# Encoder layer start: projections of half the tokens taken on unscaled x, first weight loaded in halves, third projection pair ahead of the memory's

## The chip, the cores and the metric

The kernel runs on one core of one Trainium2 chip. The metric is the device time of one execution in microseconds (us), as the median of several runs. Matrix products run on TensorE (PE, with PEld for its weight loads), elementwise work on VectorE (DVE), ScalarE (ACT) and GpSimd (POOL), and SyncE (SP) issues most of the loads.

## The reference, cut to what matters

Two encoder layers act on x (512 tokens by 1024). Each begins with a root-mean-square norm and one large input projection that feeds neighbourhood attention (A), dilated attention (B) and attention into 256 memory tokens (M):

```python
mem_n = rms_norm(mem, mem_norm_g)
for l in range(DEPTH):
    h = rms_norm(x, g_pre_mix[l])          # x * rsqrt(mean(x*x) + eps) * g
    proj = h @ w_in[l]
    q_a, k_a, v_a, q_b, k_b, v_b, q_m, gate_pre = jnp.split(proj, splits, axis=-1)
    ...
    o_m = memory_attention(q_m, mem_n, w_mem_kv[l])
    ...
```

The factor `rsqrt(mean(x*x) + eps)` is one number for each token. It can therefore be applied to h before the product or to a token's column of the product behind it. The change rests on that.

## The kernel before, in words

x lies transposed in SBUF: 8 tiles (k = 0 to 7) of 128 features, and the 512 tokens stand along the row, in two halves of 256 (`HALVES`). Every fp32 operand is split in two parts, hi (a cast by ACT, `split`, L225) and lo (a subtraction by DVE or POOL), and one product becomes three matmuls (`mm3`, L257): hi by hi, hi by lo, lo by hi. A projection of 128 output features has 8 tiles k, so it is 24 matmuls over 512 tokens, or 24 over each half of 256.

The order of TensorE's work is fixed by hand. `Woven` (L46) keeps a clock in units of TensorE work. Side jobs such as norms, softmax steps and attention heads are generators with due times on that clock, and they are put between the matmuls of the main line whenever they fall due (`tick`) or are asked for (`need`). The engines then work through their instructions in that program order and wait on semaphores, so a matmul whose operand is late holds up every matmul behind it.

At the start of layer 0 the order is this. `load_x` (L195) issues the four loads of the first half of x on SP's queue, then two weights of 512 KB follow (`group_weights`, L504), then the second half of x, the vectors and four more weights. `idle` (L883) gives TensorE products without use before data is there. `first_squares` (L871) squares a half of x on ACT and adds pairs on DVE. `rstd_job` (L334) sums the squares over the features by matmuls with a column of 1/1024, takes the square root on ACT and the reciprocal on DVE, and spreads the factor over the partitions with two transposes. `pre_norm_job` (L373) then makes h for each k: one DVE operation with x, gain and factor (`normed`, L354), the cast on ACT, the subtraction on DVE. Only then do the projections of that half start (`run_group`, L510): six weights, by pairs, into six PSUM banks, first for half 0 and then for half 1. The norm of half 1 is made beside the products of half 0. `mem_norm_job` (L460) does the same for the memory, and `mem_kv` (L488) takes its four products of 24 matmuls over 256 columns. Behind them come the third pair's projections (`proj`, L525, for `pr == 2`), with the six heads of attention A woven in (`attention_job`, L773; `a_head_job`, L608). The weights of `proj` and `mem_kv` go through two buffers for hi and two for lo (`weights`, L230).

In the profile L255 is the line of all matmuls, L266 and L351 are transposes, and L114 is the line of all DVE and ACT instructions, since a helper issues them. Tile names: `o`, `pt`, `mm`, `s` are PSUM banks, `h` and `ka` hold parts of h or x, `m` and `whi`/`wlo` hold parts of weights, `wraw` a weight as loaded, `y` squares or softmax rows.

Of the kernel before, what the change touches and what calls it, by code (L numbers as in the profile page):

```python
# [1 line left out]

# [117 lines left out]
def tile_hybrid_encoder(ctx, tc, xT, memT, memg, vecs, rpb, w_in, w_kv, w_bra, w_brb, w_brm,  # L120
# [20 lines left out]
    def nm(s):  # L141
        uid[0] += 1
        return f"{s}_{uid[0]}"
# [14 lines left out]
    def small(tag, bufs, shape=(128, 256)):  # L158
        return tp.tile(list(shape), F32, tag=tag, name=nm(tag), bufs=bufs)
# [42 lines left out]
    load_x(HALVES[0])  # L202
# [27 lines left out]
    def weights(src, K, C, slot=None, eng=None, after=None):  # L230

        raw = wp.tile([128, K, C], F32, tag="wraw", name=nm("wraw"))
# [89 lines left out]
    def sumsq_add(acc, src, first, slot=None, eng=None):  # L322
        if first:
            ACT.activation(acc, src, AF.Square)
        else:
            n = acc.shape[-1]
            sq = slot((128, 256)) if slot else small("sq2", 4) if n == 256 else small("sq", 2, (128, 512))
            ACT.activation(sq, src, AF.Square)
            (eng or V).tensor_add(acc, acc, sq)
# [40 lines left out]
        V.tensor_mul(y, ps, R)  # L370
        return y

    def pre_norm_job(l, goff, acc, hs, i, after=None):  # L373
        half, box = HALVES[i], []
        yield from rstd_job(acc if isinstance(acc, list) else [acc[:, half]], 256, box, after)
        for k in range(KD):
# [80 lines left out]
        return [(htile(), htile()) for _ in range(KD)]  # L457


    def mem_norm_job(l, hm, slot):  # L460
        raws = []
        for k2 in range(KD // 2):
            t = slot(F32, (128, 2, N_MEM))
            nc.scalar.dma_start(out=t, in_=memT[:, 2 * k2:2 * k2 + 2, :])
            raws += [t[:, 0, :], t[:, 1, :]]
        acc = small("h32", 3)
        for k in range(KD):
            sumsq_add(acc, raws[k], k == 0, None, MSQ if l else V)
        yield 14.0
        box = []  # L470
        yield from rstd_job([acc], N_MEM, box)
        for k in range(KD):
            t = slot(F32R, (128, 2, N_MEM))
            normed(raws[k], mg[:, k:k + 1], box[0], t[:, 0, :], t[:, 1, :])
            hm.append((t[:, 0, :], t[:, 1, :]))
        yield 1.2
        wv.give(f"mem{l}")

# [6 lines left out]
        vm.append(t)  # L485
        wv.give(f"vm{l}.{len(vm)}")

    def mem_kv(l, hm, km, vm, pre=()):  # L488
        wv.need(f"mem{l}")
        for m in range(4):  # L490
            w = pre[m] if pre else weights(w_kv[l, m], KD, 128)
# [15 lines left out]
    def group_banks():  # L507
        return [mmbank(), mmbank(), obank(128), tbank(), sbank(), sbank()]
# [13 lines left out]
                    mm3(ps[:, cols or half], w[k], rhs, k == 0, k == n - 1, 256)  # L522
                wv.tick()

    def proj(l, m, hs, after=None):  # L525
        w = weights(w_in[l, m], KD, 128, after=after)
        ps = mmbank()
        linear(ps, w, hs)
        return ps
# [341 lines left out]
    def first_squares(half):  # L871
        sqs = [ytile((128, 256)) for _ in range(KD)]
        for k in range(KD):
            ACT.activation(sqs[k], xh(k, half), AF.Square)
            if k % 2:
                V.tensor_add(sqs[k], sqs[k], sqs[k - 1])
            if k in (3, 5) and half != HALVES[0]:
                V.tensor_add(sqs[k], sqs[k], sqs[k - 2])
        return sqs[1::2] if half == HALVES[0] else sqs[5::2]

    idle_bank = obank(128)

    def idle(n):  # L883

        one, none = mean[:, 0:1], zero[:, 0:1]
        a, b = (bass.AP(t.tensor, t.offset, [list(t.ap[0]), [0, w]]) for t, w in ((one, 128), (none, 512)))
        for _ in range(n):
            mm(idle_bank, a, b, True, True, 0.0)

    idle(2)  # L890
    hs = h_tiles()
    sqs = first_squares(HALVES[0])
    first_copy.clear()
    gw = group_weights([w_in[0, FIRST[0]]], (V,))
    wv.spawn(pre_norm_job(0, V_PRE, sqs, hs, 0, first_copy[0]))
    gw += group_weights([w_in[0, FIRST[1]]], (V,))
# [3 lines left out]
    wv.need(f"h0.{V_PRE}.0")  # L900
    with tc.issue_after(last_copy[0]):
        sqs = first_squares(HALVES[1])
    wv.spawn(pre_norm_job(0, V_PRE, sqs, hs, 1), SD1)
    gw += group_weights([w_in[0, m] for m in FIRST[2:]], (V, G, V, G))
    for t, c in ((tab0, c_tab0), (tab1, c_tab1)):
        nc.sync.dma_start(out=t, in_=c)
    hm = []
    wv.spawn(mem_norm_job(0, hm, big), 6.0)
    km, vm = [], []

    for l in range(depth):
        pss = group_banks()
        run_group((gw, pss), hs, HALVES[0], f"h{l}.{V_PRE}.0")
        if l == 0:
            run_group((gw, pss), hs, HALVES[1], f"h{l}.{V_PRE}.1")
# [9 lines left out]
        qkva, qkvb, qm, oa, ob, om = ([], [], []), ([], [], []), [], [], [], []  # L925
        wv.spawn(attention_job(l, qkva, qkvb, qm, km, vm, oa, ob, om))
        for pr in range(3):
            for i, evac in enumerate((a_q, a_k, a_v)):
                ps = pss[FIRST.index(3 * i + pr)] if pr < 2 else proj(l, 3 * i + pr, hs, fence if i < 2 else None)
                evac(ps, qkva, *([f"va{l}.{pr}"] if i == 2 else []))  # L930
            if pr == 1:
# [202 lines left out]
```

## Time and profile before

| | before |
|---|---|
| median of 3 runs | 1534.44 us (1533.58 to 1535.34) |
| the profiled execution | 1534.84 us, of which 1533.1 us are the span from the first to the last instruction |
| TensorE busy | 1517.0 us, 99% of the span, 7970 matmuls |
| VectorE, ScalarE, GpSimd busy | 939.6, 714.0, 122.0 us |
| granted TensorE clock, mean | 0.996 |
| chain that ended last | PE 98%, DVE 1% |
| first matmul of a projection | 11.88 us after the span's start |

The profile has a page of totals and views that answer questions. In a timeline each row has the start, the duration, the engine, the line and the operation with its output and inputs; behind it stands the idle time before it and what ended that. In the chain of waits a row has the start, the time that passed, and the engine. In the table of stretches each engine has its busy time with its number of instructions, then come the granted TensorE clock, the DMA share and GB/s. In a table of groups the two numbers behind the bar are the busy time in us and the mean duration in ns. TensorE is full from about 27 us on, so what can be gained by order alone lies in front of that; what can be lost lies anywhere.

### The profile page before, as it was taken

The page shows a single profiled execution, that of the slowest core. Times are in us where ns is not written, and L with a number is a line of the kernel's source. Part 1 is how long each engine was busy: PE and PEld are TensorE (multiplying, and loading weights), DVE is VectorE, ACT ScalarE, POOL GpSimd, SP SyncE. Part 2 cuts the span into 40 slices and gives each one's busy share as a digit, 9 for nine tenths or more (in the row PEclk, how much of TensorE's full clock was granted, in tenths as well). Part 3 has the DMA queues.
Part 4 walks back from the last instruction along what each step waited for, and adds up shares of the span by engine and source line. Part 5 has one row for each costly group of instructions (what it writes and reads, how often), then busy time and mean ns, then how long its engine had stood idle before and what let it go on. Part 6 is the DMA issues. An engine that isn't in the chain of part 4 may idle for free.

```text
span 1533.1 us, 20644 instructions
## 1 busy us (share of the span) xinstructions
PE 1517.0 (99%) x7970; PEld 1297.8 (85%) x7970; DVE 939.6 (61%) x1686; ACT 714.0 (47%) x1274; POOL 122.0 (8%) x191
## 2 busy tenths in 40 slices
PE   8999999999999999999999999999999999999997
PEld 7988888888988888888898888888889888888887
DVE  6685666335777777633387856643457877776233
ACT  5565555336544444533366655532364544444231
POOL 3220000220000000010043100012100000000000
PEclk9999999999999999999999999999999999999998
DMA  7231122234112222333362222132340223223331
GB/s 255 95 112 61 62 71 97 83 96 166 55 56 96 96 99 97 118 100 98 115 180 81 87 69 71 59 103 76 117 165 15 96 97 97 96 96 90 100 106 63
DMA packets 47490, 149.23 MB, mean 97 GB/s; under 512 B 5648, under 2 KB 9872, under 8 KB 47392
## 3 DMA queue, kind: packets, MB, share of 16 engines
q1 hardware_dynamic: 43632, 139.46, 27.9%
q0 software_dynamic: 2464, 6.36, 1.6%
q10 hardware_dynamic: 1296, 2.10, 0.5%
q8 instruction: 62, 1.02, 0.3%
q14 instruction: 36, 0.29, 0.1%
HBM read 145.80 MB, written 2.10 MB: 96 GB/s over the span
## 4 chain that ended last, share of the span: by engine, by line
PE 98%; DVE 1%; DMA 0%; SPq 0%; ACT 0%; issue 0%; ACTq 0%
PE mm L255 85%; PE s L255 5%; PE o L255 4%; PE pt L266 2%; PE pt L255 2%; DMA x<-in_xT_dram 0%; DVE y L114 0%; DVE h L114 0%; PE pt L351 0%; DVE m L114 0%; SPq L198 0%; DVE x L114 0%; ACT whi L114 0%; PE s L266 0%; SPq L233 0%
## 5 line engine op out<-in xcount | busy, mean ns | idle before, releaser
L255 PE MATMUL mm<-h,whi 128*128 128x512 f32 x2496 | 775.8, 392 | 0.0
L255 PEld LDWEIGHTS mm<-h,whi 128*128 128x128 f32 x2496 | 461.1, 188 | 91.0
L255 PE MATMUL mm<-h,wlo 128*128 128x512 f32 x1248 | 486.6, 390 | 0.0
L114 DVE TENSOR_TENSOR wlo<-wraw,whi 128x1024 fp32r<-128x1024 f32 (+1 forms) x213 | 258.1, 1212 | 275.8 <-ACT whi L114 273.2
L114 ACT CAST whi<-wraw 128x1024 fp32r<-128x1024 f32 (+1 forms) x213 | 221.2, 1039 | 297.4 <-PE mm L255 284.7
L255 PEld LDWEIGHTS mm<-h,wlo 128*128 128x128 f32 x1248 | 234.2, 188 | 49.5
L255 PE MATMUL mm<-m,whi 128*128 128x512 f32 (+1 forms) x768 | 209.1, 359 | 0.0
L255 PEld LDWEIGHTS mm<-m,whi 128*128 128x128 f32 x768 | 136.9, 189 | 21.6
L255 PE MATMUL mm<-m,wlo 128*128 128x512 f32 (+1 forms) x384 | 137.6, 358 | 0.0
L114 DVE SCALAR_TENSOR_TENSOR y<-y,vec,y 128x511 f32<-128x511 f32 x176 | 130.5, 748 | 3.5 <-ACT y L114 0.9
L114 DVE TENSOR_TENSOR y<-mm,R 128x512 f32<-128x512 f32 x82 | 56.4, 688 | 68.5 <-PE mm L255 68.5
L255 PEld LDWEIGHTS mm<-m,wlo 128*128 128x128 f32 x384 | 72.4, 189 | 10.8
L114 ACT ACTIVATE y<-y,vec 128x512 f32<-128x512 f32 x88 | 71.0, 813 | 2.1 <-DVE y L114 1.9
L808 POOL TENSOR_TENSOR m<-m,y 128x512 f32<-128x512 f32 x28 | 36.1, 1289 | 397.0 <-DVE y L114 397.0
L114 ACT CAST m<-pt 128x512 fp32r<-128x512 f32 (+2 forms) x74 | 39.1, 534 | 49.6 <-PE pt L266 42.5
L114 ACT ACTIVATE y<-y 128x512 f32<-128x512 f32 x44 | 27.8, 632 | 72.3 <-DVE y L114 71.9
L255 PE MATMUL mm<-m,m 128*128 128x512 f32 x240 | 61.5, 393 | 0.0
L114 DVE TENSOR_TENSOR m<-pt,m 128x512 fp32r<-128x512 f32 (+2 forms) x74 | 45.9, 622 | 23.9 <-ACT m L114 23.1
L114 ACT ACTIVATE y<-y,st 128x256 f32<-128x256 f32 (+1 forms) x80 | 43.6, 546 | 30.7 <-DVE st L114 29.7
L114 DVE TENSOR_TENSOR acc<-acc,sq 128x256 f32<-128x256 f32 (+1 forms) x80 | 38.2, 478 | 27.4 <-ACT sq L114 25.5
L114 ACT CAST m<-y 128x512 fp32r<-128x512 f32 x32 | 19.8, 619 | 72.5 <-DVE y L114 72.5
L255 PEld LDWEIGHTS mm<-m,m 128*128 128x128 f32 x240 | 44.2, 188 | 8.8
(161 smaller groups left out, 1778.4 us busy)
## 6 DMA issues: line engine op xcount, KB each, us to landing
wraw<-in_w_in_dram SPq DMA_DIRECT2D x88, 512.0 KB, 3.7
wraw<-in_w_up_dram SPq DMA_DIRECT2D x88, 512.0 KB, 3.7
wraw<-in_w_down_dram SPq DMA_DIRECT2D x32, 512.0 KB, 3.5
wraw<-in_w_out_dram SPq DMA_DIRECT2D x16, 512.0 KB, 3.8
wraw<-in_w_down_dram SPq DMA_DIRECT2D x16, 384.0 KB, 3.1
wraw<-in_w_kv_dram SPq DMA_DIRECT2D x8, 512.0 KB, 4.1
y<-in_rpb_dram POOLq DMA_DIRECT2D x12, 256.0 KB, 3.4
wraw<-in_w_bra_dram SPq DMA_DIRECT2D x16, 192.0 KB, 2.3
```

The costliest lines, as they stand in the source:

```text
L114: return op(*args, **kw)
L255: wv.pe(nc.tensor.matmul(ps, a, b, start=first, stop=last), cost)
L266: wv.pe(nc.tensor.transpose(ps[:, 128 * i:128 * i + 128], s, ident), 0.11)
L808: (V if br == 2 and m >= 6 else G).tensor_add(acc[m], acc[m], gs)
```

## The change

Layer 0 alone is changed, and in it what stands ahead of attention B.

- The first weight is loaded in two halves between the tiles of x (`load_x` with `w`), and the first half of x is multiplied by the gain and split without its norm factor (`lead`). The six projections of half 0 run on these tiles (`raw`). Three products without use stand ahead of them, in place of two.
- The squares of half 0 are made behind the splits of the first four weights, the factor R comes from `factors_job`, and each of the six PSUM results is multiplied by R on DVE (`times_factors`). The fourth to sixth weights are loaded into buffers of other tags, so that all six loads are issued early; all six weights are split by ACT and DVE (before, two of them by ACT and POOL).
- The norm of half 1 is due later (`SDR`), and h of half 0, which the later projections need, is made behind it.
- Half 1 runs its first two weights by pair, as before, then the third pair's weights are loaded (`third`), then the other four. The memory's squares wait for h of half 0 (flag `"tiles"`). The third pair's projections come ahead of `mem_kv`, and the attention job starts after a delay (`KV_TIME`), so that the memory's products now lie among the heads of attention A.

```diff
-SD1 = 4.0
+MD0, SDR, KV_TIME = 8.0, 14.0, 16.4
...
-    def load_x(half):
+    def load_x(half, w=None, src=None):
         for k in range(0, KD, 2):
             i = half.start // 256
             nc.sync.dma_start(out=xs[:, i, k:k + 2, :], in_=xT[i, k // 2])
+            if w is not None and k % 4 == 2:
+                c = slice(k - 2, k + 2)
+                nc.sync.dma_start(out=w[:, c, :], in_=src[:, c, :])
...
-    idle(2)
+    idle(3)
     hs = h_tiles()
-    sqs = first_squares(HALVES[0])
...
+    raw = [(t[:, 0, :], t[:, 1, :]) for t in [ktile(F32R, (128, 2, 256)) for _ in range(KD)]]
+    def lead(n=2):
+        for k in [left.pop(0) for _ in range(n)]:
+            hi, lo = raw[k]
+            ACT.activation(hi, xh(k, HALVES[0]), AF.Copy, scale=g0[:, k:k + 1])
+            V.scalar_tensor_tensor(out=lo, in0=xh(k, HALVES[0]), scalar=g0[:, k:k + 1], in1=f32(hi),
+                                   op0=ALU.mult, op1=ALU.subtract)
+    gw = [[]]
+    for k in (0, 4):
+        lead(4)
+        hi, lo = big(), big()
+        split(w0[:, k:k + 4, :].rearrange("p a b -> p (a b)"), hi, lo)
...
+    for m, where in zip(FIRST[1:4], (("wraw", 3), ("wraw", 3), ("whi", 2))):
+        gw.append(weights(w_in[0, m], KD, 128, big, V, None, where))
     load_x(HALVES[1])
...
+    with tc.issue_after(last_copy[0]):
+        sqs, R = first_squares(HALVES[0]), rtile()
+    wv.spawn(factors_job(), MD0)
...
+    wv.spawn(pre_norm_job(0, V_PRE, sqs1, hs, 1), SDR)
...
+    for i in (0, 2, 4):
+        run_group((gw[i:i + 2], pss[i:i + 2]), raw, FULL, None, HALVES[0], 1 if i == 0 else 2)
+        if i == 2:
+            times_factors(0, low)
+    wv.need(f"h0.{V_PRE}.1")
+    for i in (2, 4):
+        times_factors(i, last_lo[V])
+    wv.spawn(mem_norm_job(0, hm, big, "tiles"), 0.0)
+    wv._step()
+    for k in range(KD):
+        normed(xh(k, HALVES[0]), g0[:, k:k + 1], R[:, HALVES[0]], hs[k][0][:, HALVES[0]], hs[k][1][:, HALVES[0]])
...
         fence = crit[0]
-        if l == 0:
-            mem_kv(l, hm, km, vm)
-        wv.spawn(attention_job(l, qkva, qkvb, qm, km, vm, oa, ob, om))
+        wv.spawn(attention_job(l, qkva, qkvb, qm, km, vm, oa, ob, om), 0.0 if l else KV_TIME)
...
+        if l == 0:
+            mem_kv(l, hm, km, vm, after=fence)
```

Three places show how the order moves. The first is TensorE at the start of the program. In the rows `o` is the bank of the products without use, `pt` that of the sums of squares (`mean,y`) and their transposes (`ident,st`), `mm_283` and `mm_262` the bank of the first projection. Before:

```order
L255 MATMUL o_108<-zero,mean 128x512 x2
L255 MATMUL pt_173<-mean,y_128 128x1 x2
L255 MATMUL pt_173<-mean,y_130 128x1 x2
L255 MATMUL pt_173<-mean,y_132 128x1 x2
L255 MATMUL pt_173<-mean,y_134 128x1 x2
L351 MATMUL pt_173<-ident,st_182 128x128 x2
L255 MATMUL mm_283<-h_111,m_149 128x256
L255 MATMUL mm_283<-h_112,m_149 128x256
L255 MATMUL mm_283<-h_111,m_150 128x256
```

And now:

```order
L260 MATMUL o_111<-zero,mean 128x512 x3
L260 MATMUL mm_262<-ka_131,m_147 128x256 x2
L260 MATMUL mm_262<-ka_131,m_148 128x256
L260 MATMUL mm_262<-ka_132,m_147 128x256 x2
L260 MATMUL mm_262<-ka_132,m_148 128x256
```

The sums of squares of half 0 no longer stand ahead of the first projection; they come 78 matmuls later, inside the second pair of weights.

The second place is DVE ahead of the weights that follow the six projections. `wlo` is the lo part of such a weight: of the memory before, of the third pair now. `h_95` and `h_104` collect the memory's squares, `ka` and `m_587` are evacuations of projections. Before:

```order
L114 TENSOR_TENSOR h_95_393<-h_95_393,sq_101_410 128x256
L114 TENSOR_TENSOR h_95_393<-h_95_393,sq_102_413 128x256
L114 TENSOR_TENSOR wlo_701<-wraw_698,whi_700 128x1024
L114 TENSOR_TENSOR wlo_742<-wraw_739,whi_741 128x1024
L114 RECIPROCAL st_551<-st_551 128x2
```

And now:

```order
L115 TENSOR_TENSOR m_587<-mm_262,m_587 64x512
L115 TENSOR_TENSOR h_104_521<-h_104_521,sq_107_529 128x256
L115 SCALAR_TENSOR_TENSOR ka_595<-mm_263,ka_593 64x512
L115 TENSOR_TENSOR h_104_521<-h_104_521,sq_108_532 128x256
L115 TENSOR_TENSOR wlo_615<-wraw_612,whi_614 128x1024
L115 TENSOR_TENSOR h_104_521<-h_104_521,sq_109_535 128x256
L115 TENSOR_TENSOR wlo_621<-wraw_618,whi_620 128x1024
L115 TENSOR_TENSOR h_104_521<-h_104_521,sq_110_538 128x256
L115 TENSOR_TENSOR m_726<-s_267,m_726 64x512
L115 TENSOR_TENSOR h_104_521<-h_104_521,sq_111_541 128x256
```

The memory's seven adds stood in one run (the last two are shown); they now alternate with evacuations and with the third pair's weights, and all of them stand behind the norm of half 1, the multiplications by R and h of half 0.

The third place is TensorE at the memory's products (`mm_786`, `pt_745` before, `mm_971` now); `s_984` are scores of the first head of attention A. Before:

```order
L255 MATMUL pt_745<-m_598,whi_741 128x256 x2
L255 MATMUL pt_745<-m_598,wlo_742 128x256
L255 MATMUL pt_745<-m_603,whi_741 128x256 x2
L255 MATMUL pt_745<-m_603,wlo_742 128x256
L255 MATMUL mm_786<-m_568,whi_782 128x256 x2
```

And now:

```order
L260 MATMUL mm_971<-m_792,whi_967 128x256 x2
L260 MATMUL mm_971<-m_792,wlo_968 128x256
L260 MATMUL s_984<-ka_592,m_586 128x256
L260 MATMUL s_984<-ka_594,m_586 128x256
L260 MATMUL s_984<-ka_592,m_586 128x256
L260 MATMUL s_984<-ka_594,m_586 128x256
L260 MATMUL mm_971<-m_797,whi_967 128x256 x2
L260 MATMUL mm_971<-m_797,wlo_968 128x256
```

The memory's products stood alone; now the first two heads run among them.

More of the change, by code (lines that the diff above doesn't have):

```diff
@@ L1 @@
+import contextlib
 import heapq
@@ L228, in split, with weights @@
         last_lo[eng or V] = (eng or V).tensor_sub(lo, src, f32(hi)).ins
-    def weights(src, K, C, slot=None, eng=None, after=None):
-        raw = wp.tile([128, K, C], F32, tag="wraw", name=nm("wraw"))
+    def weights(src, K, C, slot=None, eng=None, after=None, where=("wraw", 3)):
+        raw = wp.tile([128, K, C], F32, tag=where[0], name=nm("wraw"), bufs=where[1])
         nc.sync.dma_start(out=raw, in_=src)
@@ L371, in scaled, with pre_norm_job @@
         return y
-    def pre_norm_job(l, goff, acc, hs, i, after=None):
+    def pre_norm_job(l, goff, acc, hs, i, after=None, R=None):
         half, box = HALVES[i], []
         yield from rstd_job(acc if isinstance(acc, list) else [acc[:, half]], 256, box, after)
+        if R is not None:
+            ACT.copy(R[:, half], box[0])
         for k in range(KD):
@@ L465, in mem_norm_job @@
             raws += [t[:, 0, :], t[:, 1, :]]
+        if flag:
+            yield flag
         acc = small("h32", 3)
-        for k in range(KD):
-            sumsq_add(acc, raws[k], k == 0, None, MSQ if l else V)
-        yield 14.0
+        with tc.issue_after(crit[0]) if flag else contextlib.nullcontext():
+            for k in range(KD):
+                sumsq_add(acc, raws[k], k == 0, None, MSQ if l else V)
+        yield 15.5 if flag else 14.0
         box = []
@@ L475, in mem_norm_job @@
             hm.append((t[:, 0, :], t[:, 1, :]))
+        if flag:
+            with tc.issue_after(last_copy[0]):
+                ACT.activation(smalls(1), eps, AF.Exp)
         yield 1.2
@@ L486, in mem_v_job, with mem_kv @@
         wv.give(f"vm{l}.{len(vm)}")
-    def mem_kv(l, hm, km, vm, pre=()):
+    def mem_kv(l, hm, km, vm, pre=(), after=None):
         wv.need(f"mem{l}")
         for m in range(4):
-            w = pre[m] if pre else weights(w_kv[l, m], KD, 128)
+            w = pre[m] if pre else weights(w_kv[l, m], KD, 128, after=after)
             ps = (mmbank if pre or m % 2 == 0 else tbank)((128, N_MEM))
@@ L523, in run_group, with proj @@
                 wv.tick()
-    def proj(l, m, hs, after=None):
-        w = weights(w_in[l, m], KD, 128, after=after)
+    def proj(l, m, hs, after=None, w=None):
+        w = w or weights(w_in[l, m], KD, 128, after=after)
         ps = mmbank()
@@ L868, in sublayer_end, with first_squares @@
                 wv.spawn(end_job(l, goff, og, acc, acc2, i, None if then is None else (lambda i: then(acc2, i)), lat[i], more))
-    def first_squares(half):
+    def first_squares(half, between=None):
         sqs = [ytile((128, 256)) for _ in range(KD)]
@@ L878, in first_squares, with idle @@
                 V.tensor_add(sqs[k], sqs[k], sqs[k - 2])
+            if between and k in (3, 7):
+                between()
         return sqs[1::2] if half == HALVES[0] else sqs[5::2]
     idle_bank = obank(128)
-    def idle(n):
+    def idle(n, w=512):
         one, none = mean[:, 0:1], zero[:, 0:1]
-        a, b = (bass.AP(t.tensor, t.offset, [list(t.ap[0]), [0, w]]) for t, w in ((one, 128), (none, 512)))
+        a, b = (bass.AP(t.tensor, t.offset, [list(t.ap[0]), [0, w]]) for t, w in ((one, 128), (none, w)))
@@ new lines, in tile_hybrid_encoder @@
+    left = list(range(KD))
+    def lead(n=2):
[9 more added lines that the diff above has]
+        split(w0[:, k:k + 4, :].rearrange("p a b -> p (a b)"), hi, lo)
+        gw[0] += [(hi[:, 128 * i:128 * i + 128], lo[:, 128 * i:128 * i + 128]) for i in range(4)]
@@ new lines, in tile_hybrid_encoder, with factors_job @@
+    for m, where in zip(FIRST[1:4], (("wraw", 3), ("wraw", 3), ("whi", 2))):
+        gw.append(weights(w_in[0, m], KD, 128, big, V, None, where))
+    load_x(HALVES[1])
+    def factors_job():
+        box = []
+        yield from rstd_job(sqs, 256, box)
+        ACT.copy(R[:, HALVES[0]], box[0])
+    with tc.issue_after(last_copy[0]):
+        sqs, R = first_squares(HALVES[0]), rtile()
+    wv.spawn(factors_job(), MD0)
+    for m, where in zip(FIRST[4:], (("whi", 2), ("wlo", 2))):
+        gw.append(weights(w_in[0, m], KD, 128, big, V, None, where))
@@ L898, in tile_hybrid_encoder @@
+    with tc.issue_after(last_copy[0]):
+        sqs1 = first_squares(HALVES[1])
+    wv.spawn(pre_norm_job(0, V_PRE, sqs1, hs, 1), SDR)
+    low = last_lo[V]
     nc.sync.dma_start(out=vec, in_=vecs)
     nc.gpsimd.tensor_scalar_mul(hb, vec[:, :, V_BG:V_CW], 0.5)
[L900 to L908, printed above, removed]
+    pss, hm = group_banks(), []
+    def times_factors(i, after):
+        with tc.issue_after(after):
+            for ps in pss[i:i + 2]:
+                V.tensor_mul(ps[:, HALVES[0]], ps[:, HALVES[0]], R[:, HALVES[0]])
+    for i in (0, 2, 4):
+        run_group((gw[i:i + 2], pss[i:i + 2]), raw, FULL, None, HALVES[0], 1 if i == 0 else 2)
+        if i == 2:
+            times_factors(0, low)
@@ L909, in tile_hybrid_encoder @@
+    wv.need(f"h0.{V_PRE}.1")
[3 more added lines that the diff above has]
+    wv._step()
+    for k in range(KD):
+        normed(xh(k, HALVES[0]), g0[:, k:k + 1], R[:, HALVES[0]], hs[k][0][:, HALVES[0]], hs[k][1][:, HALVES[0]])
+    crit[0] = last_copy[0]
+    wv.give("tiles")
     km, vm = [], []
     for l in range(depth):
-        pss = group_banks()
-        run_group((gw, pss), hs, HALVES[0], f"h{l}.{V_PRE}.0")
+        qkva, qkvb, qm, oa, ob, om = ([], [], []), ([], [], []), [], [], [], []
+        if l > 0:
+            pss = group_banks()
+            run_group((gw, pss), hs, HALVES[0], f"h{l}.{V_PRE}.0")
@@ L914, in tile_hybrid_encoder @@
         if l == 0:
-            run_group((gw, pss), hs, HALVES[1], f"h{l}.{V_PRE}.1")
+            run_group((gw[:2], pss[:2]), hs, HALVES[1], f"h{l}.{V_PRE}.1")
+            a_q(pss[0], qkva)
+            a_k(pss[1], qkva)
+            third = [weights(w_in[l, 3 * i + 2], KD, 128, after=crit[0]) for i in range(2)]
+            for t, c in ((tab0, c_tab0), (tab1, c_tab1)):
+                nc.sync.dma_start(out=t, in_=c)
+            run_group((gw[2:], pss[2:]), hs, HALVES[1], f"h{l}.{V_PRE}.1")
```

18 lines of the change are left out of this document (8 added, 10 removed).

## The prediction

> **What bounds the kernel now.** I read the chain of waits first, over the first 140 us. Its rows have start, time passed, engine:
>
> ```profile
> 22.66 0.61 PE pt L255 x4
> ...
> 24.55 0.64 PE o L255 x3
> ...
> 37.34 5.04 PE mm L255 x42
> 42.38 0.34 PE pt L255 x4
> 42.72 0.82 PE mm L255 x6
> ...
> 44.25 0.22 PE pt L351 x2
> ...
> 49.52 5.76 PE s L255 x48
> ...
> 69.31 5.47 PE mm L255 x24
> ```
>
> A matmul of 256 columns takes 5.76/48 = 0.12 us, one of 512 columns 5.47/24 = 0.228 us. A sum of squares counts as four records here and costs 0.34 plus the 0.10 by which the next six exceed 0.72: 0.11 each. Two transposes cost 0.22. From about 27 us every row follows at this pace, so TensorE has no gap to win there. What can be won lies in front, and I measure it as **lost time**: the end of a stretch less its matmuls at this pace. At 55.28 us (49.52 + 5.76) both halves, the squares of half 1 and the memory's are done: 288 x 0.12 + 8 x 0.11 + 0.22 + 4 x 0.11 + 0.22 = 36.32 us of work. Lost: 18.96 us.
>
> Where they went shows in the timeline:
>
> ```profile
> 0.95 3.78 PE L255 MATMUL o<-zero,mean 128*128 128x512 f32 x4 [0.95 <-POOL zero L209]
> 3.40 1.41 ACT L114 ACTIVATE y<-x 128x256 f32<-128x256 f32 x4 [0.73 <-DMA x<-in_xT_dram]
> 6.36 1.36 ACT L114 ACTIVATE y<-x 128x256 f32<-128x256 f32 x4 [1.56 <-DMA x<-in_xT_dram]
> 8.27 0.62 ACT L114 CAST m<-wraw 128x512 fp32r<-128x512 f32 x1 [0.55 <-DMA wraw<-in_w_in_dram]
> 11.88 0.58 PE L255 MATMUL mm<-h,m 128*128 128x256 f32 x1 [1.17 <-ACT h L114]
> 13.38 6.56 PE L255 MATMUL mm<-h,m 128*128 128x256 f32 x41 [0.92 <-DVE h L114]
> ```
>
> The first projection waits until 11.88 us for a norm that had to wait for x, and the sums of squares of half 1 get their last operand from DVE only at 22.66 us, with nothing else for TensorE before. The third loss is the clock. Granted clock is the last number but two in the stretches; the groups give the mean duration of a matmul from 13.4 to 15.4 us and from 31.5 to 37 us:
>
> ```profile
> 23.25:23.50 0.25, 0.25 (x4) 0.25 (x4) 0.00 (x0) 0.19 (x2) 0.00 (x0) 0.76 0.16 49
> 23.50:24.00 0.50, 0.50 (x4) 0.50 (x4) 0.17 (x1) 0.50 (x3) 0.00 (x0) 0.50 0.67 131
> 26.75:27.00 0.25, 0.25 (x4) 0.25 (x4) 0.25 (x2) 0.18 (x1) 0.00 (x0) 0.91 0.53 164
> L255 PE MATMUL mm<-h,m 128*128 128x256 f32 x9 | 2.3, 434 | 0.9 <-DVE h L114 0.9
> L255 PE MATMUL s<-h,m 128*128 128x256 f32 x47 | 5.8, 283 | 0.0
> ```
>
> Half clock from about 23.4 to 26.8 us, and 0.64/3 = 0.213 us a matmul instead of 0.12. The 434 ns at 14 us are those of the slow state too (283 is the fast one), though the clock column says 1.00 there: TensorE also starts slow, until about 16.5 us.
>
> **The change part by part.** For the steps of DVE and ACT I use these durations; distances between starts are what a queue of them costs:
>
> ```profile
> 12.30 0.69 DVE L114 TENSOR_TENSOR m<-wraw,m 128x512 fp32r<-128x512 f32 x1
> 12.90 0.42 DVE L114 TENSOR_TENSOR h<-h,h 128x256 fp32r<-128x256 f32 x1
> 13.24 0.48 DVE L114 SCALAR_TENSOR_TENSOR h<-x,g,pt 128x256 f32<-128x256 f32 x1
> 13.63 0.42 DVE L114 TENSOR_TENSOR h<-h,h 128x256 fp32r<-128x256 f32 x1
> 9.66 1.64 ACT L114 CAST m<-wraw 128x512 fp32r<-128x512 f32 x3
> 17.80 2.56 ACT L114 ACTIVATE y<-x 128x256 f32<-128x256 f32 x8
> 39.35 1.98 ACT L114 CAST whi<-wraw 128x1024 fp32r<-128x1024 f32 x2
> 40.57 2.36 DVE L114 TENSOR_TENSOR wlo<-wraw,whi 128x1024 fp32r<-128x1024 f32 x2
> 44.20 0.68 DVE L114 SCALAR_TENSOR_TENSOR ka<-mm,ka 64x512 fp32r<-64x512 f32 x1 [0.98 <-ACT ka L114]
> 44.80 1.25 DVE L114 SCALAR_TENSOR_TENSOR h<-m,mg,pt 128x256 f32<-128x256 f32 x3
> 10.00:15.00 5.00, 2.89 (x10) 2.20 (x11) 4.70 (x11) 2.93 (x7) 0.56 (x1) 1.00 1.06 398
> ```
>
> So on DVE a weight quarter-megabyte split costs 0.60, a product with gain and factor 0.39, a subtraction or add 0.34, an evacuation of 64x512 0.60, a whole weight 1.18; on ACT a cast 0.51, a square 0.32.
>
> *Loads.* The second half of x reached ACT at 6.36, the first weight at 8.27 us; the half weight now takes the slot of the third load (6.36), x is complete at about 7.6, the second half weight at 8.3. At 398 GB/s each further 0.52 MB weight adds 1.3: 9.6, 10.9, 12.2, then x's second half to 14.8, the last two weights 16.1 and 17.4. All are ahead of their casts.
>
> *Start.* The lead's gain products and subtractions run under those loads. The third idle product ends at 0.95 + 3.78 x 1.5 = 6.6, before the first cast ends (6.36 + 0.62 = 7.0), so it costs nothing. The lo part of the first half weight follows at 7.7; twelve matmuls then wait for the second half weight: cast to 9.0, four lo tiles of x and the lo part on DVE to 9.95. From there twelve more reach 11.2 and the second weight 14.05. DVE and ACT have weights three and four ready at 14.2. Thirty matmuls later, at 17.65, come the squares of half 0, finished on ACT at 13.4 + 8 x 0.32 = 15.9, so without a wait. They now cost TensorE 16 records x 0.11 = 1.76, and the transposes 0.22, that before lay in front of the first product. Pair two ends at 21.8.
>
> *Pair three.* ACT's square root, and so the casts of weights five and six behind it on its queue, waits for these sums (19.4); the copy of R waits for the transposes (21.1). Weight six is split at 23.0, and TensorE waits 0.5. The squares of half 1 follow on ACT (25.5) and DVE (26.5): another 0.5. Half 0 ends at 29.85 us, against 37.34.
>
> *Half 1.* Its transposes now stand six matmuls before that end, so its h is no longer made in advance: product 0.39 x 3 on DVE, cast, subtraction: the second matmul waits until 30.9, a stall of 0.95. From then DVE's 0.73 for each k (0.39 + 0.34) against TensorE's 0.72 keep step. Half 1 ends at 36.5 + 11.5 = 48.1.
>
> *Behind it.* DVE's list from 29.3 to the last of the memory's adds is 16 products (6.2), 16 subtractions (5.4), four multiplications by R (0.38 each as between the two, 1.5), six evacuations (3.6), two weights (2.4), seven adds (2.4), about 21.6, with small waits for ACT 22.3: 51.6 us. TensorE wants the third pair's lo part at 48.5 (there at 48.85) and the memory's sum at 49.8: it waits 0.3 and then 1.9. At 52.15 the work done is 34.56 + 1.10 + 6 x 0.228 + 0.44 = 37.47, so 14.7 us are lost. **Saved: 18.96 - 14.7 = 4.3.**
>
> *Heads.* The memory's products give attention A other neighbours. Before, a head showed between its last transposes and its values work like this, never with a wait:
>
> ```profile
> 86.66 0.44 PE pt L266 x4
> 87.10 0.48 PE s L255 x4
> 87.58 1.38 PE mm L255 x6
> 88.96 0.48 PE s L255 x4
> ```
>
> That is 2.34 us of cover. In the new order the fourth head has two transposes, four scores and three matmuls, 0.22 + 0.48 + 0.68 = 1.38; the first has 2.1, but ACT has a weight's cast and two exponentials ahead of the split it needs. Between nothing and 1.2 us; I take 0.5. The number of matmuls is unchanged but for the idle one, and nothing behind attention moves.
>
> Sum: 4.3 - 0.5 = 3.8 less than the profiled execution's 1534.84, which is 0.4 above the median: **1531.0 us**.
>
> **The rivals.** *The clock stays slow (25%).* The idle products and small sums before did not free it by 14 us. If three idle products don't either, or if TensorE's half-empty 6.6 to 10 us throttle it again, up to 3.4 us of the stretch from 10 us on (23.4 to 26.8 in the trace) run at 0.213: 16 matmuls x 0.093 = 1.5, and 0.6 before. Against it: five and a half busy microseconds ahead. Result 1531.0 + 2.1 = 1533.1. [...]
>
> *DVE is not behind (20%).* If squares and adds of the memory reach TensorE in time, the 0.3 and 1.9 go: 1528.8. For it: DVE's list is a chain of small estimates, 10% less of 22.3 us covers the wait.
>
> *Slower (10%): weights behind softmax.* A weight's buffer is free only when the second product before is done; then cast (1.0) and subtraction (1.2) take 2.2, against 2.88 for one memory product and some 0.9 of scores and transposes woven in. Now ACT's exponentials of the first two heads stand in the same queue, and
>
> ```profile
> 80.00:100.00 20.00, 20.00 (x111) 17.16 (x110) 16.01 (x44) 12.67 (x32) 4.87 (x8) 1.00 0.32 103
> ```
>
> DVE was at 80% with heads among projections of 5.47 us each; it now gets a weight every 2.88. Above 1.6 us in the queue each of the four products waits; at 3.3 in the queue it is 1.7 each, 6.8 in all: 1537.8.
>
> *The early start doesn't come (5%).* If half-size loads arrive no earlier than the whole weight did, the first products wait for 8.3 + 1.6, and all later steps move by 2 to 4: about 1534.5.
>
> **How the numbers follow.** Forecast 40%, rivals 25, 20, 10 and 5. A measurement here tells 0.2% (3.07 us) from nothing. The bound for faster is 1531.4: the forecast, whose own parts vary by about 1 us to either side, counts 25 of its 40 as faster, with the 20: 45%. Within 0.2%: the other 15, the clock's 25, the 5: 45%. Slower: 10%. The range holds forecast, full cover with no loss at the heads (1528.3) and slow clock up to the late start (1535.0).
>
> **What would show it.** In the new profile: first projection at 7 us, a pause before 10; squares of half 0 inside the second pair without a gap; end of half 0 near 30 and of half 1 near 48; a wait of TensorE for DVE's memory sum of about 2 us near 50; matmuls of 283 ns from the first on. A wait at the heads above 1.2 us, matmuls of 430 ns after 10 us, or half 0 ending after 33 us would make it wrong.

## The result, and the profile after

| | before | after |
|---|---|---|
| median | 1534.44 us (5 runs, 1533.51 to 1535.34) | 1542.66 us (5 runs, 1541.56 to 1545.1) |
| profiled execution, span | 1534.84, 1533.1 | 1541.56, 1539.8 |
| granted TensorE clock, mean | 0.996 | 0.996 |
| ratio after to before | | 1.0058, 95% interval 1.0047 to 1.007 |

The change made the kernel 8.2 us slower. The forecast was 1531.0, with a range up to 1535.0, so the sign was wrong and the range too narrow. The two profiled executions lie only 6.7 us apart, since that of after is the fastest of its five; the account below is of these 6.7 us. This is the chain of waits of the changed kernel up to the first heads (start, time passed, engine):

```profile
10.34 4.30 PE mm L260 x34
...
17.85 2.03 PE pt L260 x19
...
53.31 0.58 PE pt L260 x4
53.89 1.70 PE mm L260 x6
55.59 0.43 PE pt L356 x2
56.01 3.71 PE mm L260 x11
59.79 1.05 ACT whi L115
60.87 0.95 DVE wlo L115
62.01 1.09 DVE m L115 x3
63.10 0.80 DVE h L115 x2
64.03 0.63 PE pt L271 x4
64.66 12.50 PE mm L260 x48
...
81.41 2.87 PE pt L260 x24
```

The first rows are the start as forecast: fast matmuls from 10.3 us (34 in 4.30, that is 0.126 each), the squares of half 0 among the second pair. The memory's sum comes at 53.31 instead of 51.7. Then stands a stretch that no step of the prediction has: from the end of the third pair's first product the chain leaves TensorE for ACT, DVE and DVE again, and comes back at 64.03 with four transposes.

The timeline of TensorE of the changed kernel shows its waits in brackets:

```profile
6.72 0.50 PE L260 MATMUL mm<-ka,m 128*128 128x256 f32 x2 [1.53 <-ACT m L115]
...
31.12 5.90 PE L260 MATMUL mm<-h,m 128*128 128x256 f32 x47 [0.29 <-DVE h L115]
...
49.83 0.50 PE L260 MATMUL mm<-h,wlo 128*128 128x512 f32 x1 [0.82 <-DVE wlo L115]
...
53.31 0.58 PE L260 MATMUL pt<-mean,h 128*128 128x1 f32 x4 [2.29 <-DVE h L115]
...
59.77 0.60 PE L271 MATMUL pt<-ident,sq 128*128 128x128 f32 x4
64.03 0.63 PE L271 MATMUL pt<-ident,sq 128*128 128x128 f32 x4 [3.66 <-DVE h L115]
...
91.22 0.44 PE L271 MATMUL s<-ident,m 128*128 128x128 f32 x2 [0.49 <-ACT m L115]
```

The two rows at 59.77 and 64.03 are the transposes of the first two v's (`sq`) into two banks `pt`. The first set runs at once. The second waits 3.66 us for DVE's `h`, a product that has nothing to do with v: it is the memory's norm. What the two share is a bank. There are two `pt` banks; one had just been taken by the first set, the other held the memory's norm factor until DVE's last product with it. DVE's timeline of the changed kernel shows why that product was late:

```profile
58.24 1.26 DVE L115 SCALAR_TENSOR_TENSOR h<-m,mg,pt 128x256 f32<-128x256 f32 x3
60.87 1.23 DVE L115 TENSOR_TENSOR wlo<-wraw,whi 128x1024 fp32r<-128x1024 f32 x1 [1.37 <-ACT whi L115]
62.01 1.09 DVE L115 TENSOR_TENSOR m<-h,m 128x256 fp32r<-128x256 f32 x3
63.01 0.87 DVE L115 SCALAR_TENSOR_TENSOR h<-m,mg,pt 128x256 f32<-128x256 f32 x2
```

Between the sixth and the seventh of the eight products DVE waits for a weight: the lo part of the third pair's v. Its hi part (`59.79 1.05 ACT whi`, in the chain) could only be cast when TensorE had finished with the buffer, at the end of the third pair's first product. So TensorE waited for a bank, behind DVE, behind ACT, behind TensorE's own last product.

The table of stretches gives the second new cost. The columns are the stretch, its length, busy time of PE, PEld, DVE, ACT and POOL, and the granted clock:

```profile
51.57:54.98 3.41, 1.67 (x10) 1.50 (x10) 3.09 (x6) 1.01 (x4) 0.75 (x2) 1.00 0.74 245
58.39:61.81 3.42, 1.98 (x11) 1.45 (x9) 2.05 (x4) 1.96 (x4) 0.00 (x0) 1.00 0.00 0
61.81:65.22 3.41, 1.19 (x8) 1.09 (x9) 2.89 (x8) 1.68 (x3) 0.00 (x0) 1.00 0.51 153
54.98:58.39 3.41, 3.41 (x11) 2.63 (x10) 2.34 (x7) 1.19 (x3) 0.00 (x0) 0.50 0.03 11
65.22:68.64 3.42, 3.42 (x10) 2.68 (x9) 1.61 (x4) 2.36 (x7) 0.00 (x0) 0.50 0.00 1
```

Behind each of the two waits the clock was halved for 3.4 us. The granted clock fell at 54.98 and 65.22 us and came back at 58.39 and 68.64, steps that lie 3.41, 6.83 and 3.42 us apart; a window below is such a stretch of 3.41 us, counted in a profile from its own clock steps. From 53.89 to 59.77 stand 18 matmuls of 0.228 and two transposes, 4.32 us of work in 5.88; from 64.66 on 48 matmuls, 10.94 us in 12.50. Each drop cost 1.56 us.

The account: at 53.89 TensorE had done 37.47 us of work, so 16.4 us were lost against 18.96 before, a gain of 2.5. Behind that it lost 1.56 (clock), 3.8 (from 60.2, where the first four transposes end at their usual 0.44 us, to 64.03), 1.56 (clock) and about 1.0 at the first heads. That is 7.9 us, less the 2.5 gained: 5.4 us behind. A product of 24 matmuls that both kernels have at the first attention's end shows what stood there; in the chain of waits of before:

```profile
161.56 5.46 PE mm L255 x24
```

and in that of after:

```profile
167.38 5.46 PE mm L260 x24
```

5.8 us later. So 0.4 us of that is not placed, and of the 6.7 us in the span another 0.9 arose behind it (0.2 by 1005 us, 0.7 behind the last matmul); I did not pursue them.

### The profile page after: what moved, and what is told of

Same layout as the page of the kernel before. It is cut to its first block, busy times and chain, and to the rows that moved or that the text cites. A ratio compares the mean times of both kernels' runs of the same rounds, so it can differ in the third digit from the quotient of the medians.

```text
span 1539.8 us, 20655 instructions
## 1 busy us (share of the span) xinstructions
PE 1517.9 (99%) x7972; PEld 1295.6 (84%) x7972; DVE 945.5 (61%) x1704; ACT 718.2 (47%) x1283; POOL 116.0 (8%) x187
## 4 chain that ended last, share of the span: by engine, by line
PE 97%; DVE 1%; ACT 1%; issue 0%; DMA 0%; SPq 0%; ACTq 0%
PE mm L260 84%; PE s L260 5%; PE o L260 4%; PE pt L271 2%; PE pt L260 1%; DVE h L115 0%; DVE m L115 0%; DMA x<-in_xT_dram 0%; PE pt L356 0%; DVE y L115 0%; DVE wlo L115 0%; ACT m L115 0%; ACT y L115 0%; ACT whi L115 0%; ACT ka L115 0%
## 5 line engine op out<-in xcount | busy, mean ns | idle before, releaser
L115 DVE TENSOR_TENSOR m<-pt,m 128x512 fp32r<-128x512 f32 (+2 forms) x74 | 45.7, 622 | 24.5 <-ACT m L115 23.9
L115 DVE TENSOR_TENSOR m<-wraw,m 128x512 fp32r<-128x512 f32 (+1 forms) x64 | 40.8, 655 | 23.1 <-ACT m L115 23.1
```

Of the source, the lines that this page charges most:

```text
L115: return op(*args, **kw)
```

## The experiments

The theory: the start is worth what it saved (2.5 us), and the loss is a queue of waits on one `pt` bank, with a clock drop behind each long wait. The rivals: DVE or ACT lack time as such, so that each wait taken away comes back elsewhere; or the new neighbours of the heads cost it. The kernel before was timed in each group of runs again (medians 1534.3 to 1535.0), so the ratio is what compares.

**The bank (factor_out).**

```python
+        if flag:
+            factor = acctile()[:, 0:N_MEM]
+            ACT.copy(factor, box[0])
+            box[0] = factor
         for k in range(KD):
             t = slot(F32R, (128, 2, N_MEM))
             normed(raws[k], mg[:, k:k + 1], box[0], t[:, 0, :], t[:, 1, :])
```

> The change, with one edit: the memory's norm factor is copied from its PSUM bank to SBUF by one ACT copy, and the eight norm products on DVE read the copy, so the bank is free right behind the copy. Theory (the bank): the second set of v transposes waited 3.66 us at 60.4 us for the bank that the factor held until DVE's last norm product, and the idle time then halved the clock for 3.4 us at 65.2 us, 1.5 us more. Both go: 5.2 less than the change's 1542.66, about 1537.5; up to 1 us of that may be lost again at the first heads, whose ACT and DVE work does not come earlier. Rival (the transposes wait for DVE's list as such, by any path): the stall only moves to the next matmuls that need DVE, and the time stays within 1 us of 1542.7.

Measured: 1537.71 us, ratio 1.0016 (1.0006 to 1.0025). TensorE's timeline and the stretch behind it:

```profile
61.28 0.93 PE L271 MATMUL pt<-ident,sq 128*128 128x128 f32 x7
```

```profile
65.00:68.50 3.50, 3.50 (x17) 2.90 (x16) 1.64 (x5) 3.42 (x6) 0.00 (x0) 1.00 0.33 125
```

The transposes run in one row without a wait, though DVE's subtraction stands in the norm as before, and the clock stays at 1.00 there. One copy took away 5 of the 8 us: the wait was for the bank. Profile against profile it is 3.9 us, about the wait alone: here the half clock behind the memory's sum lasted two windows (53.2 to 60.0 us), so slow clock cost as much in all as in the profile of the change.

**What held the bank (v_after).**

```python
+        last_mem[0] = last_copy[0]
...
-hs, fence if i < 2 else None,
+hs, fence if i < 2 else last_mem[0] if l == 0 and pr == 2 else None,
```

> The change, with one edit: the cast of the third pair's v weight is ordered behind the last cast of the memory's norm on ACT, so its subtraction stands behind the norm on DVE too; the bank stays as it is. Theory (the bank, held by a subtraction that waits in the middle of the norm): the norm's last product no longer waits for a weight buffer, ends at about 60.9 us instead of 63.9, the stall shrinks from 3.66 to about 0.6 us and the second clock drop goes: 4.6 less, about 1538.1. Rival (DVE has too much to do up to there, wherever the subtraction stands): the stall shrinks by the 1.14 us of the subtraction alone, 2.5 us stay and the clock drops again: about 1541.5.

Measured: 1538.61 us, ratio 1.0026 (1.0015 to 1.0037). TensorE's timeline:

```profile
60.84 0.60 PE L271 MATMUL pt<-ident,sq 128*128 128x128 f32 x4
62.85 0.63 PE L271 MATMUL pt<-ident,sq 128*128 128x128 f32 x4 [1.40 <-DVE h L115]
```

The wait fell from 3.66 to 1.40, between the theory's 0.6 and the rival's 2.5, and the time by 4 us, close to the theory's 1538.1. So both ends of the chain are shown: without the bank's hold, or without the weight in the middle of the norm, the stall is gone or short.

**Idle time and clock (warm_stall).**

```python
         yield ready(LAT_V)
+        if flag == "va0.1":
...
+            for w in (512, 512, 512, 256):
+                mm(bank[:, 0:w], a, b[:, 0:w], True, True, 0.0)
         vs.append(...)
```

> The change, with products without use (3 of 512 columns and one of 256, into the empty bank o) put on TensorE between the two sets of v transposes, where it stood idle for 3.66 us; nothing else is changed, and the wait stays. Theory (the idle time itself lowers the clock): the half clock from 65.2 to 68.6 us goes and the time falls by 1.5 to about 1541.1; the earlier drop at 55.0 us stays. Rival (the clock drop comes from something else, such as the weights' casts or the 512-column products behind it): no change, 1542.7.

Measured: 1541.54 us, ratio 1.0042 (1.0027 to 1.0057). The stretches:

```profile
55.00:58.50 3.50, 3.50 (x12) 2.81 (x12) 1.10 (x3) 0.26 (x1) 0.61 (x1) 0.50 0.31 121
...
65.00:68.50 3.50, 2.87 (x15) 2.15 (x14) 2.07 (x6) 2.54 (x5) 0.00 (x0) 1.00 0.49 150
```

The drop behind the filled wait is gone, the one behind the wait that was left as it was stays (in this execution for two windows, 53.1 to 59.9 us). From 63.33 to 66.74 us TensorE was busy for 2.78 us, of which 2.31 were the products without use. In this profile, then, the clock stayed up (1.00) behind the filled wait; it is one execution. The time fell by 1.1 as the median has it, but the intervals of this run and of the change overlap: the size is read from the matmuls (1.56), not from the times.

**The late part alone (late_only)**, on the kernel before:

```python
-        if l == 0:
-            mem_kv(l, hm, km, vm)
-        wv.spawn(attention_job(l, qkva, qkvb, qm, km, vm, oa, ob, om))
+        wv.spawn(attention_job(l, qkva, qkvb, qm, km, vm, oa, ob, om), 0.0 if l else KV_TIME)
...
+        if l == 0:
+            mem_kv(l, hm, km, vm)
         for g in range(3):
```

> The kernel before, with the late part of the change alone: third pair's projections ahead of the memory's products, the attention job delayed by 16.4. Start, norms and memory norm stay as before, so the memory's norm is finished long ahead of the v transposes. Theory (the late part costs only the waits at the first heads, and the big stall needs the late memory norm of the new start): 0.5 to 1.0 more than before, 1535.2, no wait of TensorE above 0.7 us and no clock drop behind 30 us. Rival (the new neighbours of the heads cost most of it): 1538 or more.

Measured: 1535.13 us, ratio 1.0002 (0.9992 to 1.0011). The marker product stands where it did before:

```profile
161.55 5.46 PE mm L255 x24
```

The new order of third pair, memory and heads costs nothing that shows by itself: the interval runs from 1.2 us less to 1.7 us more, so a cost of 0.5 to 1.0 is not ruled out.

**The start alone (start_only)**, on the change:

```python
-            third = [weights(w_in[l, 3 * i + 2], KD, 128, after=crit[0]) for i in range(2)]
...
+        if l == 0:
+            mem_kv(l, hm, km, vm)
-        wv.spawn(attention_job(l, qkva, qkvb, qm, km, vm, oa, ob, om), 0.0 if l else KV_TIME)
+        wv.spawn(attention_job(l, qkva, qkvb, qm, km, vm, oa, ob, om))
...
-        if l == 0:
-            mem_kv(l, hm, km, vm, after=fence)
```

> The change's start alone: unscaled half 0, halved first weight, late squares, as in the change, but the memory's products ahead of the third pair and attention not delayed, as before. Theory (what the start gains it must pay back, since the memory's norm is late): half 1 ends near 48.4, TensorE waits for the sum until about 50.5 and for the first memory tile until about 54, then each tile takes DVE 0.73 us against 0.36 of TensorE, so the first product ends near 58.6 (before: 58.16), and the long idle time lowers the clock once or twice (1.5 each): 1536 to 1538. Rival (the start is good, the late part spoils it): 1532.

Measured: 1543.62 us, ratio 1.0057 (1.0044 to 1.007). TensorE's timeline:

```profile
32.28 1.17 PE L260 MATMUL mm<-h,m 128*128 128x256 f32 x6 [1.43 <-DVE h L115]
...
45.64 5.92 PE L260 MATMUL s<-h,m 128*128 128x256 f32 x48
54.31 0.58 PE L260 MATMUL pt<-mean,h 128*128 128x1 f32 x4 [2.75 <-DVE h L115]
...
56.88 1.26 PE L260 MATMUL mm<-m,whi 128*128 128x256 f32 x2 [1.01 <-ACT m L115]
```

The theory had the sign and the place, but its size was too small: half 1 ended at 51.4, not 48.4, because h now came later from DVE, and everything behind moved with it. The edit is the reason: with the late part went the orders (`after`) that kept the next weights behind h, and in DVE's queue the first two weights of the memory now stand between the products of half 1:

```profile
30.67 1.22 DVE L115 TENSOR_TENSOR wlo<-wraw,whi 128x1024 fp32r<-128x1024 f32 x1
...
32.14 1.22 DVE L115 TENSOR_TENSOR wlo<-wraw,whi 128x1024 fp32r<-128x1024 f32 x1
```

TensorE waited 1.43 us for it, and the clock was halved from 32.9 to 36.3 us (47 matmuls took 1.17 and 6.29 us, 5.90 in the change). Neither before nor the change has these 3 us, so the 1543.62 is not the price of the start. The rival falls all the same: with those 3 us taken off whole it would still be some 1540.6 (an estimate), far from 1532. The loss is at another place than in the change, though: TensorE waits for the memory's norm itself (2.75 and 1.01 us), not for a bank. I read this so: the late memory norm costs something wherever its users stand close behind it, and the late part gives them room. No run tests that by itself.

**Sum later (sum_late)**, factor_out with one number changed:

```python
-        yield 15.5 if flag else 14.0
+        yield 18.2 if flag else 14.0
```

> The change with the factor copied out of its bank, and the memory's sum of squares put four k tiles later into the third pair's first projection (12 matmuls of 512 columns, 2.74 us), with its transposes at that projection's end. Theory: TensorE's wait of 2.3 us for the last add of the memory's squares goes, since the add ends at 53.2 and the sum is now wanted at 53.6, and with the wait goes the slow clock behind it (1.5 us, or 3 where it takes two windows); nothing behind is later, because the norm on DVE starts at the same time as before. From 1537.7: 3.8 to 5.3 less, about 1533.2, so not slower than the kernel before. Rival (DVE's norm is what TensorE lacks, and a wait taken away comes back at the next matmul that needs it): 1536 or more.

Measured: 1538.12 us, ratio 1.0023 (1.0014 to 1.0031). The time is the rival's. The waits of TensorE from 40 to 90 us:

```profile
PE pt L271 <- DVE m L115: 2.5, 1, 2.5
...
```

The wait for the sum is gone, and another of 2.5 us stands at 76 us, again transposes that want a `pt` bank, again behind a weight's subtraction in DVE's queue. In DVE's timeline:

```profile
77.07 1.23 DVE L115 TENSOR_TENSOR wlo<-wraw,whi 128x1024 fp32r<-128x1024 f32 x1 [0.28 <-ACT whi L115]
78.21 0.42 DVE L115 TENSOR_TENSOR m<-pt,m 128x256 fp32r<-128x256 f32 x1
```

The row at 78.21 frees the bank; TensorE goes on at 78.77. That the norm would start at the same time also failed: its first product came at 57.98, not 56.05, since the v weight's cast now stood ahead of the factor's copy on ACT. Moving a job by 2.7 us of TensorE moved the queues of two engines. The profiled execution is one of the faster ones (1535.70 us, 2.4 below the median), its granted clock was 0.998 in the mean, and TensorE's timeline has no matmul at the pace of half clock from 6 to 165 us; what the others lost besides, no profile shows.

**POOL's copies (dma_copies)**, on factor_out:

```python
+            if eng == "dma":
+                nc.gpsimd.dma_start(out=hi[other], in_=hi[own])
+                nc.gpsimd.dma_start(out=lo[other], in_=lo[own])
+                continue
             eng.tensor_copy(hi[other], hi[own])
             eng.tensor_copy(lo[other], lo[own])
...
-            a_k(pss[1], qkva)
+            a_k(pss[1], qkva, "dma")
```

> The change with the factor copied out, and the copies of k's rows to the other half of the partitions (first two pairs) made by DMA in place of POOL; the sum stays early. Theory (POOL's copies stretched DVE's list: the four DVE steps that ran beside them took 1.4 us longer than their like): without them the last add ends at about 51.8, TensorE's wait is 0.9 in place of 2.3, and the slow clock behind it goes in most runs: 1.4 to 3 less than 1537.7, about 1535.3. Rival (DVE's list was long for another reason): the wait stays at 2.3 and the time at 1537.7.

Measured: 1536.04 us, ratio 1.001 (1.0001 to 1.0019). In DVE's timeline of the change two of the stretched steps were

```profile
48.14 1.63 DVE L115 TENSOR_TENSOR wlo<-wraw,whi 128x1024 fp32r<-128x1024 f32 x1
...
51.17 0.82 DVE L115 TENSOR_TENSOR h<-h,sq 128x256 f32<-128x256 f32 x1
```

and here they are

```profile
48.15 1.23 DVE L115 TENSOR_TENSOR wlo<-wraw,whi 128x1024 fp32r<-128x1024 f32 x1
...
50.77 0.42 DVE L115 TENSOR_TENSOR h<-h,sq 128x256 f32<-128x256 f32 x1
```

Each is at its usual length. The last add ended 0.8 us earlier (52.36, was 53.17), not 1.4, since a wait of 0.45 us for ACT came out from under the longer steps, and TensorE still waits 1.9. The steps took 1.63 and 0.82 us beside POOL's copies and 1.23 and 0.42 without them; that was worth 0.8 us of DVE.

**Both (both_fixes):** the edits of factor_out, dma_copies and sum_late together.

> The change with the factor copied out, the sum four k tiles later and the copies by DMA. Theory: with the sum late, DVE's 1.4 us no longer hold TensorE but for part of the 0.8 us wait for the third pair's first lo part: 0.3 to 0.5 less than with the late sum alone, about 1532.8. Rival: the two gains add up in full, 1531.8 or less.

Measured: 1535.95 us, ratio 1.001 (1.0001 to 1.0018). Neither came true: the 2.5 us wait of the late sum, from 75.7 us here, is in it.

**Two ways out (mended, sum_one).** Both have the factor copied and the copies by DMA. mended puts the sum three k tiles later and mends the queue; sum_one moves the sum by one k tile only:

```python
-        yield 15.5 if flag else 14.0
+        yield 17.3 if flag else 14.0     # mended; 16.6 in sum_one
...
+        v_last[0] = last_copy[0]         # mended only, behind the split of v
...
-            w = pre[m] if pre else weights(w_kv[l, m], KD, 128, after=after)
+            w = pre[m] if pre else weights(w_kv[l, m], KD, 128, after=v_last[0] if m == 3 else after)
```

> The change with the factor copied out, k's copies by DMA, the sum of squares three k tiles later (2.05 us), and the cast of the memory's fourth weight ordered behind ACT's last cast of the third pair's v, so that DVE splits that v (which frees the transposes' bank) ahead of the weight. Theory (three waits, each for a bank or a sum that stands behind other work in DVE's queue): the 1.9 us wait for the sum that was left with the DMA copies goes, no 2.5 us wait at 76 us takes its place, and no wait of TensorE above 0.8 us is left between 12 and 140 us, so no clock drop behind 12 us: 1536.0 less 1.9 and some of the clock, about 1533.7, the kernel before or 0.1% less. Rival (DVE and ACT lack time as such between 42 and 80 us): a wait of 1.5 us or more appears elsewhere in that stretch and the time stays at 1535.5 to 1536.5.

Measured: 1534.51 us, ratio 1.0 (0.9991 to 1.0009). The 2.5 us wait is gone; waits of 0.6 and 0.8 us came in its place, and none is longer between 12 and 140 us, nor did the clock fall there (0.998 in the mean, and no matmul at the pace of half clock), as the theory had it. The marker product shows it, 2.2 us ahead of before's 161.56:

```profile
159.32 5.47 PE mm L260 x24
```

The time is half-way to the rival all the same. In the profiled execution (1534.98 us) the gain went here: at the start of layer 1 ACT waits 2.19 us for a weight's load, until 772.19 us, where it waits 0.65 us in idle_four (below), and TensorE loses 1.6 us by 786 us that it doesn't lose there (from the start of the marker product to the end of the span are 1373.9 us here and 1372.3 in idle_four). dma_copies has that wait too (1.58 us). Why the load is late in some executions is open.

> The change with the factor copied out, k's copies by DMA, and the sum of squares only one k tile later (0.68 us), which leaves DVE's and ACT's order behind it as it is with the DMA copies. Theory: the wait for the sum shrinks from 1.9 to 1.2 us, nothing else moves: 0.7 less than the 1536.0 of the DMA copies, up to 1.5 more where that keeps the clock up: 1534.5 to 1535.3. Rival (as for the other run): 1536.

Measured: 1532.86 us, ratio 0.9993 (0.9984 to 1.0002), below the forecast. The stretches show that a wait of 1.2 us for the sum is left, and that the clock holds:

```profile
52.00:56.00 4.00, 2.82 (x16) 2.11 (x15) 2.91 (x6) 1.92 (x7) 1.02 (x2) 1.00 0.93 294
56.00:60.00 4.00, 4.00 (x23) 3.38 (x22) 3.70 (x10) 3.41 (x8) 0.00 (x0) 1.00 0.11 18
```

The median is 1.65 us below mended's, but the two intervals overlap, and the profiles don't show that the smaller move was the better one: the marker product stands later here than in mended, since this execution has a slow window at the start.

```profile
159.96 5.46 PE mm L260 x24
```

What is shown is that a move of one k tile made no new wait.

**The clock at the start (idle_four):** sum_one with

```python
-    idle(3)
+    idle(4)
```

> The change with the three edits of the run before (factor copied out, k's copies by DMA, sum one k tile later) and a fourth product without use at the start. In half of the profiles of the new start the clock was halved for 3.4 us somewhere between 7.6 and 12.8 us, behind TensorE's idle stretch from about 5.5 to 7.4 us. Theory (that idle stretch lowers the clock where a window of the gate falls on it): the fourth product takes 0.9 us of the idle stretch, the first projection starts no later than 7.9, the slow window at 8 to 12 us is gone from the profile, and the median falls by some 0.3 to 0.6 from 1532.86 at an equal time of the kernel before, to about 1532.4. Rival (the slow window comes from the half-empty stretch of the first projection, 7 to 10 us, or from chance): it is still seen, and the time stays at 1532.9.

Measured: 1532.86 us, ratio 0.9989 (0.998 to 0.9998). The slow window at the start is not in this profile, whose granted clock is 1.00 in every stretch from 5 to 14 us:

```profile
0.95 5.65 PE L260 MATMUL o<-zero,mean 128*128 128x512 f32 x8 [0.95 <-POOL zero L214]
7.71 0.50 PE L260 MATMUL mm<-ka,m 128*128 128x256 f32 x2 [1.10 <-ACT m L115]
```

No run shows the gate that the theory names, or what sets its windows; what was measured are clock steps that lie multiples of 3.41 us apart, as in the profile of the change (3.41, 6.83 and 3.42 us). In v_after too the clock falls at about 7.9 and 55.7 us, about 14 times 3.41 apart, and comes back at about 11.3 and 59.1 (worked out from the granted clock of its stretches). One profile cannot show that the slow window at the start is gone from all runs, since half of the others were free of it too; the median did not fall, as the rival had it, and the 0.04% between the two ratios is inside both intervals. What this version has is a time below both kernels: 9.8 us below the change, and 1.7 us (0.11%) below before. The second margin is under the 0.2% that the prediction counts as told from nothing; the interval just excludes no difference. Its marker product stands 2.4 us ahead of before's 161.56:

```profile
159.12 5.46 PE mm L260 x24
```

That is close to the 2.5 us that the change had gained by the memory's sum and gave away. It is not the same sum: here the wait for the sum is 1.2 us in place of 2.3, and the heads still wait.

## Why the prediction was wrong, point by point

- *Loads and start:* right. The first projection came at 6.72 us (forecast 7.0); the squares of half 0 ran among the second pair; TensorE waited about 0.4 and 0.3 in pair three (0.5 and 0.5); half 0's last matmuls ended near 30.1 (29.85), the second matmul of half 1 started at 31.12 (30.9), half 1 ended at 48.4 (48.1).
- *Behind it:* mechanism right, size off. TensorE waited 0.82 for the third pair's lo part (0.3) and 2.29 for the memory's sum (1.9), the latter at 53.31 instead of 51.7. DVE's list took 23.9 us in place of 22.3. Of the 1.6, 1.4 are four steps that ran beside POOL's copies, which the list had at their undisturbed lengths (0.36, 0.20, 0.42 and 0.41 us too short). Saved: 2.5, not 4.3.
- *What stands between "Behind it" and "Heads":* this is the failing step. The sum "4.3 - 0.5" has nothing for the stretch from the memory's sum to the heads; "Heads ... 0.5" was the only charge there, and it was made by durations alone: I looked at what ACT and DVE had to do, not at which buffers their work was holding. The memory's norm moved from the middle of half 1 to beside the third pair, where two sets of v transposes want the same two banks. That wait was 3.66 us where the prediction has none. factor_out and v_after show both its ends.
- *The clock:* I charged slow clock only at the start, as a rival. In the profile of the change it cost 1.56 us behind each of two waits. That a half-empty stretch was followed by 3.4 us at half clock stood in the trace of before (the 1.5 us of my own rival), from 23.38 to 26.79 us; in its table of stretches the 3.41 us up to shortly ahead of that drop are

```profile
19.84:23.25 3.41, 1.29 (x10) 1.11 (x10) 2.70 (x5) 1.03 (x3) 2.94 (x4) 1.00 0.80 264
```

  TensorE was busy for 1.29 us of 3.41 (1.32 in the 3.41 us up to the step itself), and the clock fell. My own forecast of 1.9 us of wait at 50 us would have called for such a charge, as a chance: in dma_copies a wait of 1.87 us lay across two windows (64 and 75% busy) and the clock did not fall: two matmuls of 512 columns took 0.62 us at 53.72.
- *Heads:* about 1.0 us instead of 0.5, in the queue named but not at the step named: on ACT a weight's cast, two exponentials and the split stood ahead of the copy of the memory's third product (90.78 us), and its transposes at 91.22 us are what waited.
- *Rivals:* none of the four. "Weights behind softmax" had the right sign and the right queue (its 1537.8 is 4.9 us too low), but not the place: the memory's second product runs its 24 matmuls in 2.87 us, without a wait. "The clock stays slow" did not happen in the profile of the change (34 matmuls in 4.30 us from 10.34), yet five of the other ten profiles with the new start have one slow window of 3.4 us between 7 and 13 us, as in the stretches of sum_one:

```profile
9.00:13.00 4.00, 4.00 (x23) 4.00 (x23) 3.70 (x8) 3.34 (x8) 0.00 (x0) 0.57 1.03 412
```

- *"Nothing behind attention moves":* nearly right, 0.9 of the 6.7 us in these two profiles.

## What to carry to other kernels

When a job moves later, list what it holds (a bank, a buffer of two, a place in a queue), not only how long it takes, and ask who wants that by then; here a copy of one tile out of a bank was worth 5 us. Price a wait of some 2 us inside a kernel at its length, and add the slow clock as a risk: the wait of 2.3 us for the sum was followed by one slow window (1.56 us) in the change and by two in factor_out, the wait of 2.5 us in sum_late by none. And when a wait is to be taken away, look for what the move pushes elsewhere: 2.7 us of order took one wait away and made another of 2.5 us, 0.7 us of order left 1.2 us of it and made none.

## What the hardware showed that I had not expected

- The clock halved behind windows in which TensorE had worked for a third to a half of the time. In the profile of the change the stretch with 1.98 us busy of 3.42 was followed by full clock, those with 1.67 and 1.19 of 3.41 by half clock. Busy time alone gives no limit, though: with the windows counted from the clock's own steps, 1.60 of 3.41 us in start_only (from 49.96 us) and 1.47 in both_fixes (from 76.28 us) were followed by full clock. Nor did one busy window always bring the clock back: in factor_out it stayed halved from 56.6 to 60.0 us, behind a window with 3.39 us busy.
- Four DVE steps with both operands in SBUF took 0.2 to 0.4 us longer beside POOL's copies (1.63 against 1.21 us for a weight); evacuations with one operand in PSUM did not (0.67 to 0.69 us with and without), nor did the memory's adds at 46.62 and 47.80 us (0.42 and 0.43 us) beside the copies at 46.62 (0.89 us) and 47.83 (0.86 us). With the copies made by DMA the weight took 1.23 us.
